# Float32 attention scores in two two-bank PSUM places, the convolution in the recurrent mixer's bank, and one block-diagonal sample operand

## The chip, the cores and the metric

The kernel runs on one core of one Trainium2 chip. The metric is the device time of one execution in microseconds (us); lower is better. The time before is 1830.51 us, the median of three runs.

## What is computed

One layer of a hybrid encoder for 1024 prompt tokens and 64 sample tokens of width 1024. One projection of the normed input (12 groups of 256 columns and 4 more) feeds four mixers of 256 channels each: a gated causal convolution with 31 taps, a "forgetting" softmax attention (fox), a recurrent mixer with a matrix state (HGRN2), and a stick-breaking attention (sb). Then come the output projection, an attention over 256 memory tokens, an MLP with 4096 hidden channels, and a final norm. The two attentions have 4 heads of 64 channels:

```python
def _fox_attend(q, cq, qpos, k, v, ck, kpos):
    s = jnp.einsum('bqhd,bkhd->bhqk', q, k).astype(jnp.float32) * (HEAD_DIM ** -0.5)
    s = s + jnp.swapaxes(cq, 1, 2)[..., :, None] - jnp.swapaxes(ck, 1, 2)[..., None, :]
    s = jnp.where(kpos[None, :] <= qpos[:, None], s, NEG_BIG)
    p = jax.nn.softmax(s, axis=-1)
    return jnp.einsum('bhqk,bkhd->bqhd', p.astype(v.dtype), v)
```

The stick-breaking attention replaces the softmax by a running sum of log-sigmoids from the last key backwards. Prompt queries see the prompt's keys up to their own; the 64 sample queries see 512 cached keys and their own 64.

## The kernel before, in words

**Stages.** The input is transposed to channels first and normed (lines 222 to 278). Then the mixers run (lines 280 to 966). Then come the output projection, the memory attention and the MLP (lines 982 on). All dense products split both operands into two float32r parts, so that one product is three matmuls (`mm3`, L185).

**Lanes.** In the mixer stage four Python generators, the lanes, write the program side by side: `lane_projections` (L641), `lane_attention` (L675), `lane_conv` (L709) and `lane_hgrn` (L789). A step names a nominal cost, and the lane that is furthest behind goes on (L949). This sets the order of the program and the scheduling priorities: the projections' weights and results first, then attention, the recurrent mixer, the convolution, and last the projections' products ("fillers", `products`, L307). A scheduler at build time then fixes the order on each engine by priority among what it holds ready. Each engine executes its own list in order, so an instruction that waits holds up what is behind it on its engine. Tiles of one tag share that tag's places; a new tile waits until an old one's last reader is done. The weights of the next dense products and the stores are issued on SP's queue in the same way.

**Attention** (`attend`, L512). For each pair of heads there are eight blocks of 128 queries; block i has n = 128(i+1) keys. A head's scores are a float32 product of 64 rows (its channels) by up to 512 keys, so n over 512 takes two. Head 0 lies on partitions 0 to 63, head 1 on 64 to 127. Fox adds bfloat16 products for the forget sums (`neg1`, `ckx`), and both add a mask by one more product. The chains `sb_chain` (L467) and `fox_chain` (L480) read the scores from PSUM; `key_T` (L489) transposes the result, and the product with the values follows. Scores lie in one place of one bank (tag "zs") and one of two banks (tag "zl"):

```python
def score_tile(n, h2):
    if n > 512 or h2:
        return ps_zl.tile([P, 1024], F32, name="z", tag="zl")
    return ps_zs.tile([P, 512], F32, name="z", tag="zs")
```

For n up to 512 both heads' products stand next to each other in the program. For n over 512 (blocks 4 to 7) both heads use "zl" in turn: head 1's products follow head 0's chain. The 64 sample queries (L551 to L571) take 512 cached and 64 own keys; each head has its own products, with 64 columns of weights, into its half of the partitions.

**PSUM.** Its eight banks in this stage: two for projections (`ps_mm`), two for "zl", one each for "zs", transposes and value products (`ps_tr`), the recurrent mixer (`ps_hg`) and the convolution with some small transposes (`ps_cv`).

**Convolution** (`lane_conv`). Three chunks of up to 352 prompt tokens and one of 64 sample tokens. In each, two channel tiles are gated and run through 31 taps on DVE (L733, L736). The last chunk of a group transposes its last 30 inputs into `pco` (L743), which is copied out at L747. Then `pme` (L749) sums both channel tiles over the partitions, one matmul for each tile, and `pva` (L757) does the same with the squares.

**Recurrent mixer** (`lane_hgrn`). Six blocks, three for each pair of heads. In each, seven levels (`level`, L827) make decayed keys and queries by way of the tiles `hd` and `hx` (two places each), and the tiles `phhvn`, `pz`, `pd`, `phhkn`, `po`, `pst` and `phm` follow one another in the bank of `ps_hg`.

**After the mixers.** `split_mix` (L968) loads the mixers' outputs from DRAM (`mix_d`) and splits them; the first 512 tokens are loaded early, the others at L1133. `dense_add` (L1026) multiplies them by the output weights into `pa`, the first 512 tokens first.

Of the kernel before, what the change touches and what calls it, by code (L numbers as in the profile page):

```python
# [8 lines left out]
F32 = mybir.dt.float32  # L9
F32R = mybir.dt.float32r  # L10
BF16 = mybir.dt.bfloat16
U8 = mybir.dt.uint8
AF = mybir.ActivationFunctionType
# [4 lines left out]
P = 128  # L18
# [3 lines left out]
SS = 64  # L22
# [9 lines left out]
NEG = -2.0 ** 100       # in bfloat16 too  # L32
# [8 lines left out]
# scheduling priorities: the weights and results of the projections first, their products last, as fillers  # L41
# [3 lines left out]
class Need:  # L45
    """a step of a lane that waits until a projection has been issued"""
# [6 lines left out]
def kernel(ctx: ExitStack, tc: tile.TileContext, *args):  # L53
# [25 lines left out]
    # ---------------------------------------------------------------- constants  # L79
# [27 lines left out]
    # lvl[m][s, blk] = 1 where s lies in the first half of block blk of 2m tokens  # L107
# [31 lines left out]
    # ---------------------------------------------------------------- helpers  # L139
    def rstd_chain(pool, n, mean_sq, tag, scale=1.0, parts=P, out=None):  # L140
        """1/sqrt(mean_sq*scale + eps): exp(-ln/2) and one Newton step."""
# [12 lines left out]
    def softplus_tail(out, z):  # L154
        """out = ln(1 + exp(-|z|))"""
        act(out, z, AF.Abs)
        act(out, out, AF.Exp, scale=-1.0)
        act(out, out, AF.Ln, bias=1.0)

    def sigmoid(out, z):  # L160
        """out = exp(min(z, 0) - ln(1 + exp(-|z|)))"""
        softplus_tail(out, z)
        V.scalar_tensor_tensor(out=out, in0=z, scalar=0.0, in1=out, op0=ALU.min, op1=ALU.subtract)
        act(out, out, AF.Exp)
# [20 lines left out]
    def mm3(ps, w, a, kt=KD, group=0):  # L185
        """ps = W^T a with W and a as pairs of exact float32r parts; a(k) gives the moving pair. With group set, the
        products of that many k stay together once the first is scheduled."""
# [13 lines left out]
    pj_d = dram.tile([12, P, T], F32, name="pj_d")      # cv_a, cv_g, hq, hf, hi, hgate: two tiles each  # L201
# [20 lines left out]
    # ---------------------------------------------------------------- x, channels first. The first norm's gain goes  # L222
    # into the products' operand, its 1/rms, on all partitions in rb, into their results
# [56 lines left out]
    # ---------------------------------------------------------------- projections and mixers  # L280
    ps_zl = mx.enter_context(tc.tile_pool(name="ps_zl", bufs=1, space=PSUM))
    ps_zs = mx.enter_context(tc.tile_pool(name="ps_zs", bufs=1, space=PSUM))
    ps_tr = mx.enter_context(tc.tile_pool(name="ps_tr", bufs=1, space=PSUM))
    ps_hg = mx.enter_context(tc.tile_pool(name="ps_hg", bufs=1, space=PSUM))
    ps_cv = mx.enter_context(tc.tile_pool(name="ps_cv", bufs=1, space=PSUM))
# [21 lines left out]
    def products(work):  # L307
        """the products of one chunk of a projection, as fillers"""
        ps = ps_mm.tile([P, 512], F32, name="pm", tag="mm")
        prio, tc.cur_priority = tc.cur_priority, PR_MM + pending[1]  # L310
        work(ps)
        pending[1] += 24
        tc.cur_priority = prio
        return ps
# [6 lines left out]
    def together(parts, src=w_in, moving=h_at, chunks=CH):  # L321
        """projections, chunk by chunk"""
# [6 lines left out]
    def project_narrow(c0, cols, sink):  # L329
        """projection to a few channels: the k go in turn to the four column groups of the tensor engine, side by side,  # L330
        so that channel c comes in four parts, on partitions c, 32 + c, 64 + c and 96 + c"""
# [11 lines left out]
    def natural(src, j, out_p, out_s, cs, keep=None):  # L343
        """src [128 channels, n] of chunk j -> rows to DRAM and, if asked, to keep [128, 9, 128]."""
# [13 lines left out]
    def memory_kv():  # L358
        """keys and values of the prompt memory: to the outputs, the keys also with channels first"""
# [50 lines left out]
    def project_qkv(kind, hp, cq, ck, cv, cache_k, cache_v, outs):  # L410
        """projections of one head pair as steps; the tiles land in tiles[kind, hp]"""
# [41 lines left out]
    def caches(hp, cache_k, cache_v):  # L453
        """cached keys of one head pair, channels first, and values"""
# [12 lines left out]
    def sb_chain(z, n):  # L467
        """exp(z - sum of softplus(z) over the keys from its own on). v = that sum - z runs backwards through the keys:
        v[j] = (v[j + 1] + z[j + 1]) - log_sigmoid(z[j]). The last key is masked for all: its v is -NEG, its weight 0."""
# [19 lines left out]
    def key_T(p, n):  # L489
        """p [128, n keys] -> [128 keys, n/128, 128]"""  # L490
# [16 lines left out]
    def score_tile(n, h2):  # L507
        if n > 512 or h2:
            return ps_zl.tile([P, 1024], F32, name="z", tag="zl")
        return ps_zs.tile([P, 512], F32, name="z", tag="zs")  # L510

    def attend(hp, kind, mask, chain, cache_k, cache_v, mix_slot):  # L512
# [3 lines left out]
        for i in range(8):  # L516
            n = P * (i + 1)
            # the two heads lie on different rows of the tensor engine: their products go side by side
            zs, aTs = [None, None], []

            def scores(heads):
                for h2 in heads:
                    zs[h2] = score_tile(n, h2)
                for c in range(0, n, 512):
                    for h2 in heads:
                        w = min(512, n - c)
                        mm(zs[h2][:, c:c + w], qT[hd[h2], i * P:(i + 1) * P], kT[hd[h2], c:c + w], True,
                           c + w < n and not fox)
                for h2 in heads:
                    if fox:  # L530
                        for c in range(0, n, 512):
                            w = min(512, n - c)
                            mm(zs[h2][:, c:c + w], neg1[:, 2 * hp + h2], ckx[:, c:c + w], False, c + w < n)
                    mm(zs[h2][:, n - P:n], ident_bf, mask[0], False, True)

            if n <= 512:
                scores((0, 1))
            for h2 in range(2):
                if n > 512:
                    scores((h2,))  # L540
# [12 lines left out]
        z = score_tile(n, 0)  # L553
        for h2 in range(2):
            mm(z[hd[h2], 0:PAST], qT[hd[h2], SP:T], kcT[hd[h2]], True, not fox)
            mm(z[hd[h2], PAST:n], qT[hd[h2], SP:T], kT[hd[h2], SP:T], True, False)
            if fox:
                mm(z[hd[h2], 0:PAST], neg1[:, 2 * hp + h2, 0:SS], ckx[:, SP:SP + PAST], False, True)
                mm(z[hd[h2], PAST:n], neg1[:, 2 * hp + h2, 0:SS], ckx[:, SP + PAST:], False, False)
            mm(z[hd[h2], PAST:n], ident_bf[:, hd[h2]], mask[1], False, True)  # L560
# [12 lines left out]
    # ---- log forget sums, kept as three exact bfloat16 parts so that the score products can take them in  # L573
# [5 lines left out]
    Q.memset(ckx, 0.0)  # L579
    for h in range(4):  # L580
        Q.memset(neg1[32 * h:32 * h + 3, h], -1.0)

# [17 lines left out]
    def ck_cache():  # L600
# [3 lines left out]
        ps = ps_cv.tile([P, 4, P], F32, name="plc", tag="cv")  # L604
# [6 lines left out]
    def sink_f(ps, j):  # L611
# [11 lines left out]
        def later():  # L623
            pl = ps_cv.tile([P, 4, 4], F32, name="plf", tag="cv")
# [15 lines left out]
    # ---- the projections, in the order in which the mixers ask for them  # L640
# [32 lines left out]
    # ---- the two attentions. The query's own log forget sum is the same for every key of a row: the row maximum  # L673
    # takes it out again, so that s + cq - ck - max(s + cq - ck) = (s - ck) - max(s - ck).
# [14 lines left out]
    # ---- convolution, chunk by chunk, with the last 30 gated inputs carried over  # L689
# [11 lines left out]
    ps = ps_cv.tile([P, 4, 64], F32, name="pcw", tag="cv")  # L701
# [7 lines left out]
    def lane_conv():  # L709
        tails = [None, None]  # L710
        for t0, n in [(t, min(CN, SP - t)) for t in range(0, SP, CN)] + [(SP, SS)]:
# [30 lines left out]
            if last:  # L742
                ps = ps_cv.tile([P, G], F32, name="pco", tag="cv")  # L743
# [5 lines left out]
            pm = ps_cv.tile([P, 512], F32, name="pme", tag="cv")  # L749
# [7 lines left out]
            pv2 = ps_cv.tile([P, 512], F32, name="pva", tag="cv")  # L757
# [13 lines left out]
    # ---- HGRN2: blocks of 128 tokens. With DEPTH = 1 the lower bounds are cumsum(softmax) - softmax[0] = 0 over  # L771
    # an axis of one, so that log f = log_sigmoid(z) and k = sigmoid(-z). Within a block the pairs s < t are cut by
    # halving: both sides of a pair take their decay up to the middle of the smallest block of 2m that holds both.
# [5 lines left out]
    # decayed keys, and decayed queries of each head with zeros for the other head's channels  # L779
# [3 lines left out]
    # scores, s on partitions; every s < t is written for each block, and the rest stays zero. The last place is for  # L783
    # the block of 64 tokens
# [4 lines left out]
    def lane_hgrn():  # L789
        state = {}  # L790
        step = 0
        for hp, (t0, n) in [(hp, c) for hp in range(2) for c in ((0, 384), (384, 384), (768, 320))]:
# [34 lines left out]
            def level(m):  # L827
                """decayed keys and queries of one level"""
                nonlocal step
                nn = nf * P if m == 64 else n  # L830
                dd, ex = ht("hd", bufs=2), ht("hx", bufs=2)
# [3 lines left out]
                bv, dv, xv, qv, kv, ykv, q0, q1 = (bl(a) for a in (b, dd, ex, q, kk, yk, yq[:, 0], yq[:, 1]))  # L835
                V.tensor_tensor(out=dv, in0=bv, in1=bv[:, :, m - 1:m].to_broadcast([P, nn // (2 * m), 2 * m]),
                                op=ALU.subtract)
                act(xv[:, :, m:], dv[:, :, m:], AF.Exp)
                act(xv[:, :, :m], dv[:, :, :m], AF.Exp, scale=-1.0)
# [33 lines left out]
            # s = t  # L873
# [6 lines left out]
            # k decayed to the end of its block (tokens on partitions), q decayed from its start  # L880
            ke = ht("hke", "hd", 2)[:, :n]
# [39 lines left out]
            # per-head norm and gate  # L921
# [354 lines left out]
```

## Time and profile before

| | |
|---|---|
| runs | 1829.59, 1830.51, 1832.58 us; median 1830.51 us |
| span of the profiled execution, first to last instruction | 1828.7 us (its own time is not listed apart; the three runs lie 0.9 to 3.9 us above the span) |
| TensorE (PE) busy | 1778.7 us, 97% |
| weight loads (PEld) busy | 1525.0 us, 83% |
| VectorE (DVE) busy | 1028.4 us, 56% |
| ScalarE (ACT) busy | 784.3 us, 43% |
| GpSimd (POOL) busy | 106.0 us, 6% |

How to read it: busy shares are unions of the instructions' times, and the ends of matmuls are modelled, so successive matmuls overlap in the records; what one costs in a stream is the distance from its start to the next one's. A float32 product shows as two matmul records. A tile's name stands on the left of "<-", what it is made from on the right. A wait is the idle time of an engine ahead of an instruction, put down to what came last.

### The profile page before, as it was taken

To read this page: it belongs to the slowest core of one execution; us is meant where nothing else is said; L and a number is where in the kernel's file an instruction comes from. 1 tells how busy PE (TensorE), PEld (TensorE's weight loads), DVE (VectorE), ACT (ScalarE), POOL (GpSimd) and SP (SyncE) were. 2 spreads that over 40 slices of the span, in tenths; PEclk is the share of its full clock that TensorE was granted. 3 is DMA by queue.
4 is the path that set the end of the run, shared out by engine and by line. 5 is a ranking of instruction groups with operands and counts; after the bars stand their busy time and mean duration, and the time that the engine had idled before them with its cause. 6 is when DMAs were issued, how large, how long until landed. Compare 5 with 4: busy or idle time off the path is not lost. (4 is left out here: it accounts for less than half of the span.)

```text
span 1828.7 us, 28923 instructions
## 1 busy us (share of the span) xinstructions
PE 1778.7 (97%) x11379; PEld 1525.0 (83%) x11379; DVE 1028.4 (56%) x2070; ACT 784.3 (43%) x1618; POOL 106.0 (6%) x193
## 2 busy tenths in 40 slices
PE   7999999999999999999999999999999999999997
PEld 6877757776776787988799999999999999999987
DVE  6455579878788875756867764232323232332335
ACT  6464556355446854445555361413131323232233
POOL 3010202000311300000000000000000000000000
PEclk9999999999999999999999999999999999999999
DMA  8221212222233359322322321111111111111212
GB/s 257 76 65 44 58 48 77 63 64 73 68 102 96 103 161 278 99 87 69 104 76 70 104 75 53 40 53 41 42 46 47 47 35 58 35 52 35 59 41 99
DMA packets 224311, 141.76 MB, mean 78 GB/s; under 512 B 14382, under 2 KB 213743, under 8 KB 224175
## 3 DMA queue, kind: packets, MB, share of 16 engines
q1 hardware_dynamic: 223919, 139.90, 25.8%
q8 instruction: 90, 1.47, 0.4%
q14 instruction: 46, 0.38, 0.1%
q0 software_dynamic: 256, 0.01, 0.0%
HBM read 111.97 MB, written 27.87 MB: 76 GB/s over the span
## 5 line engine op out<-in xcount | busy, mean ns | idle before, releaser
L71 PE MATMUL pu<-ap,wh 128*128 128x512 f32 (+2 forms) x1536 | 363.9, 328 | 0.1
L74 ACT ACTIVATE wh<-wr 128x1024 fp32r<-128x1024 f32 (+1 forms) x196 | 169.8, 866 | 431.4 <-PE pdn L71 286.0
L71 PE MATMUL pm<-ap,wh 128*128 128x256 f32 (+2 forms) x1408 | 340.7, 333 | 0.6 <-DVE vT L430 0.3
L71 PEld LDWEIGHTS pu<-ap,wh 128*128 128x128 f32 x1536 | 261.7, 189 | 20.7 <-DVE ap L168 0.3
L71 PEld LDWEIGHTS pm<-ap,wh 128*128 128x128 f32 x1408 | 234.6, 192 | 24.0 <-issue 3.2
L71 PE MATMUL pu<-ap,wl 128*128 128x320 f32 (+2 forms) x768 | 251.2, 327 | 0.0
L168 DVE TENSOR_TENSOR wl<-wr,wh 128x1024 fp32r<-128x1024 f32 (+1 forms) x196 | 193.2, 986 | 97.2 <-ACT wh L74 90.7
L71 PE MATMUL pm<-ap,wl 128*128 128x256 f32 (+2 forms) x704 | 226.9, 322 | 0.0
L1215 DVE TENSOR_TENSOR xT<-xT,pdn 128x512 f32<-128x512 f32 (+2 forms) x192 | 102.1, 532 | 203.0 <-PE pdn L71 203.0
L71 PE MATMUL pa<-ap,wh 128*128 128x256 f32 (+2 forms) x768 | 186.0, 331 | 1.0 <-ACT wh L74 0.6
L71 PE MATMUL pdn<-aq,wh 128*128 128x256 f32 (+1 forms) x896 | 181.2, 295 | 0.0
L71 PEld LDWEIGHTS pu<-ap,wl 128*128 128x128 f32 x768 | 145.3, 189 | 10.2
L71 PEld LDWEIGHTS pdn<-aq,wh 128*128 128x128 f32 x896 | 148.4, 189 | 4.4
L71 PEld LDWEIGHTS pa<-ap,wh 128*128 128x128 f32 x768 | 131.4, 190 | 12.3 <-ACT wh L74 1.4
L71 PEld LDWEIGHTS pm<-ap,wl 128*128 128x128 f32 x704 | 134.4, 191 | 8.3 <-DVE wl L168 0.2
L71 PE MATMUL pdn<-hid,wh 128*128 128x512 f32 x448 | 139.3, 392 | 0.0
L71 PE MATMUL pdn<-aq,wl 128*128 128x320 f32 x448 | 132.6, 296 | 0.0
L71 PE MATMUL pa<-ap,wl 128*128 128x512 f32 (+2 forms) x384 | 126.4, 330 | 0.0
L736 DVE SCALAR_TENSOR_TENSOR y<-ext,cwT,y 128x352 f32<-128x352 f32 (+2 forms) x240 | 113.7, 501 | 2.2
L74 ACT ACTIVATE rl<-pu 128x320 f32<-128x320 f32 (+2 forms) x96 | 44.8, 467 | 150.7 <-PE pu L71 150.7
L168 DVE TENSOR_TENSOR hid<-rl,hid 128x512 fp32r<-128x512 f32 x32 | 22.1, 692 | 136.8 <-ACT hid L74 136.8
L71 PE MATMUL pq<-ap,wh 128*128 128x512 f32 (+2 forms) x384 | 93.1, 331 | 0.0
(310 smaller groups left out, 2795.7 us busy)
## 6 DMA issues: line engine op xcount, KB each, us to landing
wr<-in_w_up_dram SPq DMA_DIRECT2D x36, 512.0 KB
wr<-in_w_down_dram SPq DMA_DIRECT2D x64, 256.0 KB
wr<-in_w_in_dram SPq DMA_DIRECT2D x24, 512.0 KB
wr<-in_w_out_dram SPq DMA_DIRECT2D x16, 512.0 KB
wr<-in_w_mq_dram SPq DMA_DIRECT2D x16, 512.0 KB
wr<-in_w_mo_dram SPq DMA_DIRECT2D x32, 256.0 KB
xt<-in_x_prompt_dram SPq DMA_DIRECT2D x8, 512.0 KB
wr<-in_w_mk_dram SPq DMA_DIRECT2D x8, 512.0 KB
```

The source lines that it names most:

```text
L71: nc.tensor.matmul(out, lhsT=lhsT, rhs=rhs, start=start, stop=stop, **kw)
L74: nc.scalar.activation(out=out, in_=in_, func=func, **kw)
L168: V.tensor_tensor(out=lo, in0=src, in1=hi.bitcast(F32), op=ALU.subtract)
L736: V.scalar_tensor_tensor(out=y[:, :n], in0=ext[:, j:j + n], scalar=cwT[:, ct, j:j + 1], in1=y[:, :n], op0=ALU.mult, op1=ALU.add)
L1215: V.tensor_tensor(out=xs, in0=xs, in1=ps[:, :cn], op=ALU.add)
```

## The change

Comments and doc strings are also removed; those lines are left out here. What remains:

```diff
-    ps_zl = mx.enter_context(tc.tile_pool(name="ps_zl", bufs=1, space=PSUM))
-    ps_zs = mx.enter_context(tc.tile_pool(name="ps_zs", bufs=1, space=PSUM))
+    ps_z = mx.enter_context(tc.tile_pool(name="ps_z", bufs=2, space=PSUM))
     ps_tr = mx.enter_context(tc.tile_pool(name="ps_tr", bufs=1, space=PSUM))
     ps_hg = mx.enter_context(tc.tile_pool(name="ps_hg", bufs=1, space=PSUM))
-    ps_cv = mx.enter_context(tc.tile_pool(name="ps_cv", bufs=1, space=PSUM))
...
+    def score_tile():
+        return ps_z.tile([P, 1024], F32, name="z", tag="z")
...
+            zs, aTs = [score_tile() for _ in range(2)], []
+            for c in range(0, n, 512):
+                for h2 in range(2):
+                    w = min(512, n - c)
+                    mm(zs[h2][:, c:c + w], qT[hd[h2], i * P:(i + 1) * P], kT[hd[h2], c:c + w], True,
+                       c + w < n and not fox)
+            for h2 in range(2):
+                if fox:
+                    for c in range(0, n, 512):
                         w = min(512, n - c)
...
+                        mm(zs[h2][:, c:c + w], neg1[:, 2 * hp + h2], ckx[:, c:c + w], False, c + w < n)
+                mm(zs[h2][:, n - P:n], ident_bf, mask[0], False, True)
             for h2 in range(2):
-                if n > 512:
-                    scores((h2,))
                 p = chain(zs[h2][:, :n], n)
...
+        for sl in hd:
+            act(qbd[sl, sl], qT[sl, SP:T], AF.Copy)
+        z = score_tile()
+        mm(z[:, 0:PAST], qbd, kcT, True, not fox)
+        mm(z[:, PAST:n], qbd, kT[:, SP:T], True, False)
+        if fox:
+            mm(z[:, 0:PAST], neg2[:, hp], ckx[:, SP:SP + PAST], False, True)
+            mm(z[:, PAST:n], neg2[:, hp], ckx[:, SP + PAST:], False, False)
+        mm(z[:, PAST:n], ident_bf, mask[1], False, True)
...
+    neg2 = const.tile([P, 2, P], BF16, name="neg2")
+    Q.memset(neg2, 0.0)
     for h in range(4):
         Q.memset(neg1[32 * h:32 * h + 3, h], -1.0)
+        Q.memset(neg2[32 * h:32 * h + 3, h // 2, (h % 2) * 64:(h % 2 + 1) * 64], -1.0)
+    qbd = const.tile([P, P], F32, name="qbd")
+    Q.memset(qbd, 0.0)
...
-            pm = ps_cv.tile([P, 512], F32, name="pme", tag="cv")
+            pm = ps_hg.tile([P, 512], F32, name="pme", tag="hg")
...
-                dd, ex = ht("hd", bufs=2), ht("hx", bufs=2)
+                ex = ht("hx", bufs=2)
...
-                V.tensor_tensor(out=dv, in0=bv, in1=bv[:, :, m - 1:m].to_broadcast([P, nn // (2 * m), 2 * m]),
+                V.tensor_tensor(out=xv, in0=bv, in1=bv[:, :, m - 1:m].to_broadcast([P, nn // (2 * m), 2 * m]),
                                 op=ALU.subtract)
-                act(xv[:, :, m:], dv[:, :, m:], AF.Exp)
-                act(xv[:, :, :m], dv[:, :, :m], AF.Exp, scale=-1.0)
+                act(xv[:, :, m:], xv[:, :, m:], AF.Exp)
+                act(xv[:, :, :m], xv[:, :, :m], AF.Exp, scale=-1.0)
```

All tiles of `ps_cv` (`plc`, `plf`, `pcw`, `pco`, `pme`, `pva`) move to `ps_hg` with tag "hg" in the way shown for `pme`. The tag "hd" of the recurrent mixer (`hke`, `hsq`, a part of the norm) now has one place. No DMA is added or moved.

## Rows read from the trace of the kernel before

**Rows 1.** The page: busy us (share of the span) and instructions of each engine.

```profile
PE 1778.7 (97%) x11379; PEld 1525.0 (83%) x11379; DVE 1028.4 (56%) x2070; ACT 784.3 (43%) x1618; POOL 106.0 (6%) x193
```

**Rows 2.** Windows, mixer stage: length, busy PE, PEld, DVE, ACT, POOL, clock, DMA, GB/s.

```profile
45.00:690.00 645.00, 618.27 (x4315) 469.78 (x4314) 479.82 (x994) 346.04 (x739) 88.86 (x136) 0.99 0.28 79
```

**Rows 3.** Waits of PE, mixer stage: us in total, times, longest.

```profile
PE z L71 <- DVE sba L475: 3.4, 4, 1.5
...
PE pz L71 <- POOL ky L842: 3.1, 3, 1.4
...
PE pz L71 <- DVE hsc L867: 2.2, 3, 1.4
```

**Rows 4.** Timeline of PE, prompt scores: start, us, what, count of records.

```profile
59.62 0.49 PE L71 MATMUL z<-kT,qT 64*128 64x128 f32 x4
...
70.49 0.91 PE L71 MATMUL z<-kT,qT 64*128 64x384 f32 x2
...
71.72 0.91 PE L71 MATMUL z<-kT,qT 64*128 64x384 f32 x2
...
92.45 1.12 PE L71 MATMUL z<-kT,qT 64*128 64x512 f32 x2
...
94.09 0.48 PE L71 MATMUL z<-kT,qT 64*128 64x128 f32 x2
...
555.48 0.70 PE L71 MATMUL z<-kT,qT 64*128 64x256 f32 x4
...
561.26 0.92 PE L71 MATMUL z<-kT,qT 64*128 64x384 f32 x4
```

**Rows 5.** Timeline of PE, sample scores of sb and fox.

```profile
193.84 1.07 PE L71 MATMUL z<-kv,qT 64*64 64x512 f32 x2
...
195.09 1.07 PE L71 MATMUL z<-kv,qT 64*64 64x512 f32 x2
...
481.95 1.07 PE L71 MATMUL z<-kv,qT 64*64 64x512 f32 x2
...
483.46 0.55 PE L818 MATMUL phhvn<-ident,hv 128*128 128x128 f32 x3
```

**Rows 6.** Instructions on z, last readers: ns min/median/max, first and last start.

```profile
L475 DVE TENSOR_TENSOR_SCAN sba<-z,sba x34: 396/1351/2287, 62.2 to 364.2; 128x127 f32<-128x127 f32 x4, 128x255 f32<-128x255 f32 x4, 128x383 f32<-128x383 f32 x4, 128x511 f32<-128x511 f32 x4
...
L74 ACT ACTIVATE fp<-z,fm x34: 343/742/1122, 390.7 to 658.0; 128x128 f32<-128x128 f32 x4, 128x256 f32<-128x256 f32 x4, 128x384 f32<-128x384 f32 x4, 128x512 f32<-128x512 f32 x4
```

**Rows 7.** Instructions on pco, and timeline of PE: convolution's and recurrent mixer's banks.

```profile
L745 PE MATMUL pco<-ident,ext x4: 284/285/287, 516.0 to 657.2; 128*30 128x128 f32 x4
L747 DVE COPY cvo<-pco x2: 403/403/403, 570.3 to 671.4; 30x256 f32<-30x256 f32 x2
...
574.07 0.70 PE L71 MATMUL pme<-y,ones 128*128 128x320 f32 x2
...
607.84 0.76 PE L71 MATMUL pme<-y,ones 128*128 128x320 f32 x2
...
534.14 0.49 PE L818 MATMUL phhvn<-ident,hv 128*128 128x128 f32 x3
```

**Rows 8.** Timelines of SP, DVE and PE where the mixers end.

```profile
682.29 0.61 SPq L934 DMA_DIRECT2D mix_d<-ho  x1
...
696.92 0.32 SPq L768 DMA_DIRECT2D mix_d<-y  x1
...
709.75 1.42 DVE L168 TENSOR_TENSOR ap<-aqw,ap 128x576 fp32r<-128x576 f32 x2
...
734.01 0.45 PE L71 MATMUL pa<-ap,wh 128*128 128x320 f32 x2
```

**Rows 9.** Taps of y (DVE), nearest rows to the new copies (ACT) and memsets (POOL).

```profile
L736 DVE SCALAR_TENSOR_TENSOR y<-ext,cwT,y x240: 266/556/1245, 305.9 to 682.5; 128x352 f32<-128x352 f32 x60, 128x320 f32<-128x320 f32 x30, 128x64 f32<-128x64 f32 x30
...
L74 ACT ACTIVATE os<-pvs x3: 217/224/224, 374.7 to 667.1; 128x64 f32<-128x64 f32 x3
...
L581 POOL MEMSET neg<- 3x128 bf16 x4 | 0.8, 200 | 0.2
```

More of the change, by code (lines that the diff above doesn't have):

```diff
@@ L505, in key_T @@
         return aT
[L507 to L510, printed above, removed]
+    def score_tile():
+        return ps_z.tile([P, 1024], F32, name="z", tag="z")
     def attend(hp, kind, mask, chain, cache_k, cache_v, mix_slot):
@@ L517, in attend @@
             n = P * (i + 1)
[L519 to L525, printed above, removed]
-                        w = min(512, n - c)
[L527 to L537, printed above, removed]
+            zs, aTs = [score_tile() for _ in range(2)], []
[7 more added lines that the diff above has]
+                    for c in range(0, n, 512):
+                        w = min(512, n - c)
+                        mm(zs[h2][:, c:c + w], neg1[:, 2 * hp + h2], ckx[:, c:c + w], False, c + w < n)
+                mm(zs[h2][:, n - P:n], ident_bf, mask[0], False, True)
             for h2 in range(2):
-                if n > 512:
-                    scores((h2,))
                 p = chain(zs[h2][:, :n], n)
@@ L552, in attend @@
         kcT, vc = caches(hp, cache_k, cache_v)
[L553 to L560, printed above, removed]
+        for sl in hd:
[7 more added lines that the diff above has]
+        mm(z[:, PAST:n], ident_bf, mask[1], False, True)
         p = chain(z[:, :n], n)
@@ L603, in ck_cache @@
         nc.sync.dma_start(out=lc, in_=cache_fox_logf[0, 0].rearrange("(i p) h -> p i h", p=P))
-        ps = ps_cv.tile([P, 4, P], F32, name="plc", tag="cv")
+        ps = ps_hg.tile([P, 4, P], F32, name="plc", tag="hg")
         for j in range(4):
@@ L623, in later @@
         def later():
-            pl = ps_cv.tile([P, 4, 4], F32, name="plf", tag="cv")
+            pl = ps_hg.tile([P, 4, 4], F32, name="plf", tag="hg")
             for i in range(0, n, P):
@@ L700 @@
     nc.sync.dma_start(out=hist, in_=cache_conv[0, 0])
-    ps = ps_cv.tile([P, 4, 64], F32, name="pcw", tag="cv")
+    ps = ps_hg.tile([P, 4, 64], F32, name="pcw", tag="hg")
     for ct in range(2):
@@ L742, in lane_conv @@
             if last:
-                ps = ps_cv.tile([P, G], F32, name="pco", tag="cv")
+                ps = ps_hg.tile([P, G], F32, name="pco", tag="hg")
                 for ct in range(2):
@@ L756, in lane_conv @@
                 act(sq[ct], ys[ct], AF.Square)
-            pv2 = ps_cv.tile([P, 512], F32, name="pva", tag="cv")
+            pv2 = ps_hg.tile([P, 512], F32, name="pva", tag="hg")
             for ct in range(2):
@@ L834, in level @@
                 bl = lambda a: a[:, :nn].rearrange("p (c w) -> p c w", w=2 * m)
-                bv, dv, xv, qv, kv, ykv, q0, q1 = (bl(a) for a in (b, dd, ex, q, kk, yk, yq[:, 0], yq[:, 1]))
-                V.tensor_tensor(out=dv, in0=bv, in1=bv[:, :, m - 1:m].to_broadcast([P, nn // (2 * m), 2 * m]),
+                bv, xv, qv, kv, ykv, q0, q1 = (bl(a) for a in (b, ex, q, kk, yk, yq[:, 0], yq[:, 1]))
+                V.tensor_tensor(out=xv, in0=bv, in1=bv[:, :, m - 1:m].to_broadcast([P, nn // (2 * m), 2 * m]),
                                 op=ALU.subtract)
-                act(xv[:, :, m:], dv[:, :, m:], AF.Exp)
-                act(xv[:, :, :m], dv[:, :, :m], AF.Exp, scale=-1.0)
+                act(xv[:, :, m:], xv[:, :, m:], AF.Exp)
+                act(xv[:, :, :m], xv[:, :, :m], AF.Exp, scale=-1.0)
                 V.tensor_tensor(out=q0[0:64, :, m:], in0=xv[0:64, :, m:], in1=qv[0:64, :, m:], op=ALU.mult)
@@ L879, in lane_hgrn @@
             V.tensor_tensor(out=tv, in0=vT, in1=pd[:, :n], op=ALU.mult)
-            ke = ht("hke", "hd", 2)[:, :n]
+            ke = ht("hke", "hd")[:, :n]
             for g0, gn in groups:
@@ L920, in lane_hgrn @@
             yield 3
-            sq = ht("hsq", "hd", 2)[:, :n]
+            sq = ht("hsq", "hd")[:, :n]
             act(sq, o, AF.Square)
@@ L927, in lane_hgrn @@
             nc.sync.dma_start(out=gT, in_=pj_d[10 + hp][:, t0:t0 + n])
-            r = rstd_chain(hc, n, pm[:, :n], (("hd", 2), ("hx", 2), "hz"), scale=1.0 / HD)
+            r = rstd_chain(hc, n, pm[:, :n], ("hd", ("hx", 2), "hz"), scale=1.0 / HD)
             V.tensor_tensor(out=o, in0=o, in1=r, op=ALU.mult)
```

## The prediction

> **What bounds the kernel now.** I read the page first: TensorE is busy for 97% of the span [rows 1], and no other engine comes near. Then the windows, because the change touches the mixer stage alone: from 45 to 690 us PE is busy for 618 of 645 us [rows 2], so its idle time there is only 27 us. The projections' products fill it up to the end of the stage. So the stage costs what PE has to execute, plus the idle time, unless the end of a lane comes too late. Third, the waits of PE: its idle time is spread over many small waits, of which the score products' wait for the stick-breaking scan is 3.4 us in four times and the recurrent mixer's for its operands a few us [rows 3]. A shorter wait of another engine is worth nothing here; fewer or overlapping matmuls are.
>
> Durations below come from the profiled execution, span 1828.7 us. The median of the runs is 1830.5, so 1.8 us lie around the span. I take the sum off the median.
>
> **Sample operand.** Before, each head has its own set of score products, one after the other: head 0 starts at 193.84, head 1 at 195.09, so a set costs 1.25 us in sb; in fox 481.95 to the next product at 483.46 holds head 1's set, 1.51 us [rows 5]. Afterwards one set with all 128 rows and columns does both. A set's records have the same number of moving columns, so I take the same price. Saved: 2 × 1.25 + 2 × 1.51 = 5.5 us of PE. The zeros cost nothing more as long as a product of 128 rows streams like one of 64; the bound from below is therefore 0 if the full operand took twice as long, from above 5.5. I take 5.5, because the columns are what differ between the prompt's records of 0.48, 0.91 and 1.12 us [rows 4].
>
> **Prompt scores, blocks 4 to 7.** Two heads' products that stand next to each other on PE do run side by side: block 0 has both heads' 128 columns, four records, in 0.49 us, and one head alone takes 0.48; four records of 384 columns take 0.92 and one head alone 0.91 [rows 4]. A pair costs what one head costs. One head's products in blocks 4 to 7 are four of 512 columns and one each of 128, 256, 384 and 512: 5 × 1.12 + 0.48 + 0.70 + 0.91 = 7.7 us by the records (0.70 is a pair's, which is one head's). Four attentions: 30.8 us if every block pairs.
>
> But will they pair? The program order is no guarantee, as blocks 1 to 3 show. They already have a place for each head and both heads' products next to each other in the program. Yet 384 columns of head 0 start at 70.49 and those of head 1 at 71.72, with transposes between. Of the twelve blocks 1 to 3 of the four attentions two pair, at 555.48 and 561.26 [rows 4]. The reason is in the chains: head 0's place comes free when its last reader ends, and head 1's only one such reader later, up to 2.29 us for a scan in sb and up to 1.12 us for an exponential in fox [rows 6]. Head 0's products are ready first, rank above the fillers and go alone. Two places change nothing about that for blocks 4 to 7. Bounds: 0 (no product is added, so no loss) and 30.8. I take the share of the nearest rows, 2 of 12: 5.1 us.
>
> The Trainium skill ("TensorE: Matmul & The Clock Gate", Part 3, Packing small matmuls) says that matmuls on different row groups overlap, with starts about 4 ns apart; taken for every block it makes this term 30.8 us, the second rival below; block 0's row agrees, the ten unpaired blocks show what it needs first. The Trainium skill ("TensorEngine Tiling (Array Packing)", Performance Considerations, PSUM Bottleneck) warns that packing speeds up TensorE but not the emptying of PSUM; by it this term would be 0 and the time 1826.3; ten of the twelve blocks agree, two don't.
>
> **Second place.** With one place for blocks 4 to 7, the next head's scores wait for the previous chain, 3.4 us of PE idle time in four waits [rows 3]. With two, the chain is one head further. I take half, 1.7 us; bounds 0 and 3.4. That attention gets ahead faster gains nothing else: the projections that it needs are PE work too, and it will wait for them.
>
> **One bank for convolution and recurrent mixer.** This is the price. The scheduler gives a free place to whoever is ready, and the convolution holds its tiles for long: `pme` takes its first channel tile at 574.07 and its second at 607.84, 34 us later, because 31 taps of the second lie between, each 0.56 us by the median and last in priority on DVE [rows 7, 9]. `pco` is written from 516.0 on and copied at 570.3, 54 us; the second is written by 657.2 and copied at 671.4, 14 us [rows 7]. In a shared bank the recurrent mixer stands still during such a hold, and its next tile after 516 us is needed at 534.14 [rows 7].
>
> Three things bound what that costs. (1) While it stands still, DVE has only taps and evictions to do, so the holds shrink: between 516.0 and 534.14, 18 us, DVE could do 32 of the third chunk's 62 taps if it did nothing else; I estimate 20 beside its other work, so 40 are left, 22 us, and the recurrent mixer's own first steps need no bank. I put the recurrent mixer's delay at 15 us behind the third chunk and 15 behind the fourth, 30 in all (bounds: 0, and the 54 + 34 + 14 = 102 us of the holds). (2) PE does not starve: fillers and the first 512 tokens' output projection lie behind. What must come in time is the second part of the mix: the recurrent mixer stores last at 682.29, the convolution at 696.92, the splits end near 711.2 (two from 709.75, 1.42 us), and the first product on them starts at 734.01 [rows 8]. So the recurrent mixer may be late by 697 − 682 = 15 and the whole by another 23: 38 us. 30 is under that: cost 0. (3) PE runs its list in order, and products of the recurrent mixer that now wait for the convolution's readers hold up fillers. The nearest rows are the 3.1 and 2.2 us that its products wait today [rows 3]; I take 3, bounds 0 and 8.
>
> **Nothing for the rest.** `hd` and `hx` in one tile: the subtraction of a level now waits for POOL's readers of two levels ago, some half us per level of the recurrent mixer; cover is the same 38 us, and 42 levels at 0.5 would use up to 21 of them. The eight copies into `qbd`, some 0.22 us each like `os<-pvs` [rows 9], are 1.8 us on ACT, busy for 346 of 645 us [rows 2], with fillers on PE meanwhile. Six memsets of about 0.2 us [rows 9] join POOL's start; nothing waits for POOL there but work of the mixers after 45 us; uncovered they are 1.2 us. No DMA moves, on SP or POOL.
>
> **Sum.** −5.5 − 5.1 − 1.7 + 3 = −9.3; 1830.5 − 9.3 = 1821.2 us.
>
> **Rivals.**
> 1. *No pair forms and the shared bank eats the rest.* For: the staggered release [rows 6] and 10 of 12 unpaired blocks. −5.5, no gain from the second place, +4 to +8 of waits: 1827 to 1833, say 1829. That is also the case in which the change doesn't do what it says.
> 2. *All long blocks pair.* For: a pair costs one head [rows 4], and a filler group ahead of the scores may last until both places are free. Against: the same twelve blocks. −5.5 − 30.8 − 1.7 + 3 = −35: 1795.5.
> 3. *Slower: the recurrent mixer arrives too late.* One mechanism: the holds of `pco` and `pme` in its bank, from 516 us on. It decides once its delay is over 38 us; each us beyond is paid at 734 us. For: 102 us of holds, levels that are slower by up to 21, and a chain that is short of DVE. Against: the holds shrink as DVE comes free. With half the holds and half the levels' delay, 51 + 10 = 61: 23 − 9 = +14, 1844; with the full sum of 102 it is +64 − 9 = +55, 1886.
>
> **How the numbers follow.** Forecast 45%, rival 1 18%, rival 2 12%, rival 3 25%. A measurement of this kernel can tell about 0.2%, 3.7 us, from no change: under 1826.9 is faster, over 1834.2 slower. Faster: 43 points of the forecast and all of rival 2, 55%. Same: rival 1 and the rest of the forecast, 20%. Slower: 25%. The forecast alone, with the bounds of pairing (0 to 30.8, mostly under 12) and of the waits (0 to 8), lies between 1812 and 1828. The range reaches to most of rival 3's nearer half and part of rival 2: 1802 to 1844.
>
> **What would show it.** Right: one set of `z<-kv` products for each attention's sample, a gap of 1.2 to 1.5 us closed; few four-record groups among the long blocks, with transposes of head 0 between the heads; waits of `z` on L475 below 3.4; `pco` and `pme` in the recurrent mixer's bank with holds, and its store later than 682 but the first 320-column product of `pa` without a wait and about 9 us before 734. Wrong: many pairs of 512 columns (rival 2); idle PE ahead of `pa` on the split of `aqw`, or a last mixer store after 720 us (rival 3); more idle time of PE ahead of `pz`, `po` and `pme` than the gain (rival 1).

## The result, and the profile after

The changed kernel takes 1880.68 us (median of 4 runs, 1878.28 to 1882.76) against 1830.05 us for the kernel before in the same comparison: a ratio of 1.0276, 95% interval [1.0262, 1.0291]. It is **slower by about 50 us**; the forecast was 1821.2 us, the range 1802 to 1844.

The page of the changed kernel (busy us and share, then the granted clock in 40 slices of 47 us each) answers to [rows 1]:

```profile
PE 1784.7 (95%) x11345; PEld 1532.8 (82%) x11355; DVE 1033.4 (55%) x2070; ACT 781.9 (42%) x1626; POOL 97.9 (5%) x199
...
PEclk9999986999999976999999999999999999999999
```

PE is busy 6 us longer in a span of 1876.5 us that is 48 us longer, and the clock has two dips, in slice 7 (281 to 328 us) and in slices 15 and 16 (657 to 751 us). The windows show what PE did there. First the kernel before (its first row is [rows 2]), then the changed one; the columns are length, busy PE, PEld, DVE, ACT, POOL, clock, DMA, GB/s:

```profile
260.00:330.00 70.00, 65.24 (x433) 47.68 (x434) 62.84 (x128) 40.42 (x76) 12.17 (x23) 0.98 0.27 75
690.00:735.00 45.00, 45.00 (x197) 37.27 (x196) 27.33 (x41) 22.48 (x37) 0.00 (x0) 0.97 0.91 279
```

```profile
45.00:690.00 645.00, 597.97 (x4108) 465.45 (x4116) 452.71 (x920) 328.76 (x710) 65.38 (x113) 0.95 0.28 79
260.00:330.00 70.00, 52.37 (x297) 32.75 (x298) 41.85 (x70) 36.30 (x73) 11.04 (x20) 0.67 0.09 27
690.00:735.00 45.00, 23.80 (x126) 13.81 (x127) 22.66 (x50) 12.77 (x34) 11.91 (x19) 0.50 0.09 26
```

Between 260 and 330 us PE executes 297 matmul records instead of 433. Between 690 and 735 us it is busy for 23.8 of 45 us, where before it had no idle time at all. In both stretches VectorE and ScalarE do less as well: none of the three is overloaded, they wait.

**The first stall: 260 to 326 us.** Instructions of the changed kernel on `plf` (transposes of the forget gate) and on `fl`, its input (ns min/median/max, first and last start), then those on `pm`, the projections' products, between 255 and 326 us:

```profile
L621 PE MATMUL plf<-ident,fl x9: 168/242/264, 326.2 to 332.1; 4*128 4x4 f32 x8, 4*64 4x4 f32 x1
...
L615 DVE SCALAR_TENSOR_TENSOR fl<-fz,fl x3: 388/471/680, 241.4 to 330.0; 4x512 f32<-4x512 f32 x1, 4x256 f32<-4x256 f32 x1, 4x320 f32<-4x320 f32 x1
...
L71 PE MATMUL pm<-ap,wh x8: 278/282/384, 255.2 to 256.5; 128*128 128x256 f32 x8
```

The first `fl` is written at 241.4, but its transposes start at 326.2; in the kernel before they started at 254.3. After 256.6 not one product of a projection starts until 328.5. The kernel before has these rows, on `plf` and, for 260 to 326 us, on `pm`:

```profile
L627 PE MATMUL plf<-ident,fl x9: 168/198/221, 254.3 to 265.3; 4*128 4x4 f32 x8, 4*64 4x4 f32 x1
...
L71 PE MATMUL pm<-ap,wh x136: 279/309/631, 261.7 to 323.7; 128*128 128x256 f32 x48, 128*128 128x320 f32 x48, 128*128 128x512 f32 x40
```

The code gives the link: `fl` lies in the two places (tag "st") through which the projections' results also leave. While `plf` waits for the bank, `fl` can't be given up, the results can't leave, the two PSUM places of `pm` stay full, and PE has no filler.

**The second stall: up to 782 us.** The recurrent mixer's first tile of each block is `phhvn`, the convolution's last of each chunk is `pva`. Both on PE, with first and last start: `phhvn` from 440 us on (blocks 4 to 6) in the kernel before, then `phhvn` and `pva` in the changed one:

```profile
L818 PE MATMUL phhvn<-ident,hv x9: 272/273/328, 483.5 to 614.5; 128*128 128x128 f32 x8, 128*64 128x128 f32 x1
```

```profile
L812 PE MATMUL phhvn<-ident,hv x9: 272/273/445, 632.9 to 721.3; 128*128 128x128 f32 x8, 128*64 128x128 f32 x1
...
L71 PE MATMUL pva<-sq,ones x16: 220/459/543, 404.1 to 631.2; 128*128 128x352 f32 x8, 128*128 128x320 f32 x4, 128*128 128x64 f32 x4
```

Blocks 4 to 6 no longer run beside the convolution but behind it: block 4 begins at 632.9, 1.7 us after the start of the last `pva` of the fourth chunk, and 149 us later than before. Its input `hv` had long been sent for, by the instructions on `hv` (SP) between 440 and 650 us:

```profile
L795 SPq DMA_DIRECT2D hv<-pj_d x1: 320/320/320, 490.3 to 490.3; - x1
```

The waits of PE in the whole execution (total, times, longest) show which chain is then alone. In [rows 3] `pz` had 3.1 and 2.2 and `z` 3.4; now there are

```profile
PE pz L71 <- POOL ky L836: 14.8, 4, 8.4
...
PE pz L71 <- DVE hsc L861: 8.5, 4, 3.2
PE z L71 <- DVE sba L473: 5.7, 5, 3.3
PE phhvn L812 <- DVE ho L927: 5.1, 1, 5.1
```

and the end of the mixers, on SP and on PE, answers to [rows 8]:

```profile
765.53 0.32 SPq L928 DMA_DIRECT2D mix_d<-ho  x1
...
782.09 0.45 PE L71 MATMUL pa<-ap,wh 128*128 128x320 f32 x2
```

The recurrent mixer stores last at 765.5 instead of 682.3, and the first 320-column product of `pa` starts at 782.1 instead of 734.0: 48 us, the whole difference of the spans.

**The theories.** Listed in the order in which the program asks for them, the tiles of the shared bank are: blocks 1 to 3 with `plf` and `plc` near the end of block 3, then all four chunks of the convolution, then blocks 4 to 6. Asking means here the first product or transpose that is written into the tile. The changed kernel's trace serves the bank in this order, tile for tile. So the theory is **order**: the scheduler at build time hands out the places of one tag in program order, and a tile that asks later waits even if its operands are ready and the bank is empty. The rival is the prediction's: a free place goes to whoever is ready, and it is the **length of the holds** that costs. Other rivals put the loss on the score places or on the merge of `hd` and `hx`.

### The profile page after: what moved, and what is told of

It is laid out like the page before. It is cut to its first block, busy times and chain, and to the rows that moved or that the text cites. A ratio compares the mean times of both kernels' runs of the same rounds, so it can differ in the third digit from the quotient of the medians.

```text
span 1876.5 us, 28901 instructions
## 1 busy us (share of the span) xinstructions
PE 1784.7 (95%) x11345; PEld 1532.8 (82%) x11355; DVE 1033.4 (55%) x2070; ACT 781.9 (42%) x1626; POOL 97.9 (5%) x199
```

## The experiments

### One part of the change at a time

**Sample operand (`qbd` and `neg2`) and merge alone**, on the kernel before:

```diff
+    act(qbd[sl, sl], qT[sl, SP:T], AF.Copy)
...
-    mm(z[hd[h2], 0:PAST], qT[hd[h2], SP:T], kcT[hd[h2]], True, not fox)
...
+    mm(z[:, 0:PAST], qbd, kcT, True, not fox)
...
-    dd, ex = ht("hd", bufs=2), ht("hx", bufs=2)
+    ex = ht("hx", bufs=2)
```

> The kernel before with two parts of the change alone: the block-diagonal sample operand (one set of score products for both heads) and, because the operand's two constants need the space, the merge of hd and hx. PSUM stays as it was: one two-bank and one one-bank place for scores, a bank of its own for the convolution. Theory (the loss is in the shared bank): the operand gives its 5.5 us and the merge costs nothing, about 1824.5 us against 1830. Rival (the merge makes the recurrent mixer's levels slow enough to be late): 1840 us or more. Rival (a product of 128 rows and columns takes twice as long, no gain from the operand): 1830 us.

Measured: 1822.0 us, ratio 0.9966 [0.9953, 0.9979], so 6.2 us faster (3.8 to 8.6). The operand pays what was forecast, and the merge costs nothing that shows.

**The shared bank alone**, on the kernel before; `pcw`, `plf`, `plc`, `pco` and `pva` are moved like `pme`:

```diff
-    ps_cv = mx.enter_context(tc.tile_pool(name="ps_cv", bufs=1, space=PSUM))
...
-    pm = ps_cv.tile([P, 512], F32, name="pme", tag="cv")
+    pm = ps_hg.tile([P, 512], F32, name="pme", tag="hg")
```

> The kernel before with one part of the change alone: the convolution's and the forget gate's six PSUM tiles in the recurrent mixer's bank (the freed bank stays empty). Theory (the bank's places are handed out in program order, so that blocks 4 to 6 of the recurrent mixer come after all four chunks of the convolution): the whole loss of the change without its gains, 1885 to 1895 us, and the bank served exactly in the order of the program, block 4's first tile after the last chunk's second moment. Rival (the second place of the scores, their pairing or the merge of hd and hx causes the loss): 1830 to 1838 us.

Measured: 1897.87 us, ratio 1.0378 [1.0364, 1.0392]. This one part costs 69 us, more than the whole change and 3 us more than the theory's upper end. Its `phhvn` from 440 us on and its `pva`:

```profile
L817 PE MATMUL phhvn<-ident,hv x9: 273/273/446, 649.1 to 741.8; 128*128 128x128 f32 x8, 128*64 128x128 f32 x1
...
L71 PE MATMUL pva<-sq,ones x16: 222/458/488, 422.1 to 647.1; 128*128 128x352 f32 x8, 128*128 128x320 f32 x4, 128*128 128x64 f32 x4
```

Again block 4 begins right after the last `pva`. The score places and the merge aren't the cause; the rest of the change gives 17 us back (1897.9 to 1880.7).

### Order or length of the holds

**The forget gate's tiles (`plf`, and `plc` in the same way) elsewhere**, on the changed kernel:

```diff
-    pl = ps_hg.tile([P, 4, 4], F32, name="plf", tag="hg")
+    pl = ps_mm.tile([P, 4, 4], F32, name="plf", tag="mm")
```

> The changed kernel with the forget gate's two PSUM tiles (plf, plc) moved to the two places of the projections' products; the convolution's pcw, pco, pme and pva stay in the recurrent mixer's bank. Theory (program order): plf no longer waits behind block 3 of the recurrent mixer, the products of the projections run on from 260 to 326 us where they stood still, and some 25 us come back: about 1856 us; blocks 4 to 6 still come after the last chunk. Rival (what counts is only how long the convolution holds the bank): plf and plc are short tiles, so no change, 1876 to 1885 us.

Measured: 1850.42 us, ratio 1.0118 [1.0104, 1.0133]: 30 us of the 50 are back, 6 more than expected. The window 260 to 330 us is as it was in the kernel before, clock included:

```profile
260.00:330.00 70.00, 64.78 (x475) 50.30 (x473) 65.63 (x126) 41.47 (x78) 10.50 (x21) 1.00 0.26 73
```

In the changed kernel `plf`, the tile that caused this stall, is held for less than 1 us each time, from its first write to its last reader. It was where it stood, not how long it stayed. Blocks 4 to 6 still come behind the last chunk: block 4 begins at 603.4, after a last `pva` from 599.4 to 602.9.

**The convolution later in the program**, on the changed kernel:

```diff
-             Lane(lane_conv(), 1.0, PR_CONV), Lane(lane_hgrn(), 1.0, PR_HGRN)]
+             Lane(lane_conv(), 4.0, PR_CONV), Lane(lane_hgrn(), 1.0, PR_HGRN)]
```

> The changed kernel with one number changed: the convolution's lane counts its steps four times, so that in the program its chunks 2 to 4 stand behind the recurrent mixer's blocks 4 to 6. Priorities, tiles and the length of each hold are the same. Theory (program order decides): blocks 4 to 6 start near 490 us instead of 633, the last mixer results come 20 to 40 us earlier, 1840 to 1860 us; plf still waits behind block 3, so that the stall between 260 and 326 us stays. Rival (the bank goes to whoever is ready first, and the holds cost the time): the same order of service as in the changed kernel, 1876 to 1885 us.

Measured: 1896.86 us, ratio 1.0377 [1.0363, 1.0392]. The time is a miss, 37 us over the theory's upper end, but the order of service turned round as the theory says: block 4 begins at 501.9, and the last chunk's `pva` comes at 786.3.

```profile
L812 PE MATMUL phhvn<-ident,hv x9: 272/273/273, 501.9 to 638.3; 128*128 128x128 f32 x8, 128*64 128x128 f32 x1
...
L71 PE MATMUL pva<-sq,ones x16: 218/459/486, 410.1 to 786.3; 128*128 128x352 f32 x8, 128*128 128x320 f32 x4, 128*128 128x64 f32 x4
```

Now the convolution is what arrives too late, by the timeline of SP: its last stores start at 792, not at 697.

```profile
792.22 2.00 SPq L762 DMA_DIRECT2D mix_d<-y  x2
```

The expectation had left out what it costs that chunks 2 to 4 then stand behind block 6, one after the other.

**Short holds at the old places**, on the changed kernel; `pco` is asked for and copied for each channel tile, ahead of its taps:

```diff
+    ps = ps_hg.tile([P, P], F32, name="pco", tag="hg")
...
-    for ct in range(2):
-        mm(pm[:, :n], ones, ys[ct], ct == 0, ct == 1)
+    for ct in (1, 0):
+        mm(pm[:, :n], ones, ys[ct], ct == 1, ct == 0)
```

> The changed kernel with short holds and the same places in the program's order: the convolution's means begin with the second channel tile (ready last), and pco becomes one small tile for each channel tile, copied before the taps begin. Each hold of 10 to 36 us of pme and 8 to 30 us of pco becomes one of a few us. Theory (program order decides; the previous run with the convolution's chunks behind block 6 moved block 4 from 633 to 502 us): block 4 still starts only after the fourth chunk's second moment, near 630 us, 1870 to 1883 us. Rival (the length of the holds decides): the recurrent mixer uses the bank between them, block 4 starts before 520 us, 1815 to 1835 us.

Measured: 1880.01 us, ratio 1.0295 [1.0276, 1.0314]: no change. The holds of `pme` are gone: in the changed kernel the second chunk's records lie 17 us apart, here all four stand together, timeline of PE:

```profile
470.72 0.76 PE L71 MATMUL pme<-y,ones 128*128 128x352 f32 x2
487.71 0.92 PE L71 MATMUL pme<-y,ones 128*128 128x352 f32 x2 [0.89 <-DVE y L730]
```

```profile
494.10 1.45 PE L71 MATMUL pme<-y,ones 128*128 128x352 f32 x4 [0.50 <-DVE y L736]
```

And its instructions on `phhvn` from 440 us on and on `pva`:

```profile
L810 PE MATMUL phhvn<-ident,hv x9: 272/273/445, 636.5 to 724.2; 128*128 128x128 f32 x8, 128*64 128x128 f32 x1
...
L71 PE MATMUL pva<-sq,ones x16: 275/457/563, 409.7 to 634.9; 128*128 128x352 f32 x8, 128*128 128x320 f32 x4, 128*128 128x64 f32 x4
```

From 500 to 636 us the holds, each from the first write to the last reader, sum to 23 us, 12 of them one `pva`; the bank is empty for the rest, and still block 4 begins at 636.5, behind the last `pva`. This rules the length of the holds out as what keeps block 4 back.

### The order put right

**Convolution's lane counted twice**, with the forget gate's tiles in `ps_mm`: chunk 3 falls within block 5 and chunk 4 within block 6.

```diff
-             Lane(lane_conv(), 1.0, PR_CONV), Lane(lane_hgrn(), 1.0, PR_HGRN)]
+             Lane(lane_conv(), 2.0, PR_CONV), Lane(lane_hgrn(), 1.0, PR_HGRN)]
```

> The kernel with the forget gate's tiles in the projections' places (1850.4 us), and with the convolution's lane counting its steps twice, so that in the program block 4 stands before the third chunk, the third chunk's tiles within block 5 and the fourth's within block 6, much as the kernel before served its two banks in time. Holds and priorities are the same. Theory (program order): block 4 near 490 us, block 6 done before 700 us, both lanes end within 30 us of each other, 1818 to 1832 us. Rival (any sharing of the bank with holds of 10 to 36 us costs the time whatever the order): 1845 to 1860 us.

Measured: 1825.79 us, ratio 0.9979 [0.9965, 0.9993]. Against 1850.4 the order alone gives 25 us, and the sharing now costs less than the rest of the change gains. The 45 us that were half idle are filled again, and block 4 begins at 472.3, by the window and by the instructions on `phhvn` from 440 us on:

```profile
690.00:735.00 45.00, 44.00 (x217) 36.63 (x217) 32.38 (x50) 24.05 (x41) 0.00 (x0) 1.00 0.76 234
```

```profile
L812 PE MATMUL phhvn<-ident,hv x9: 272/273/301, 472.3 to 626.5; 128*128 128x128 f32 x8, 128*64 128x128 f32 x1
```

**The same with short holds** (the two edits together):

> The run with the forget gate's tiles in the projections' places and the convolution's lane counted twice (1825.8 us), now with the short holds as well. Theory (order first, and once the order is right the remaining holds of 10 to 25 us and what waits behind them cost what is left to the run without any common bank, 16 us): 1812 to 1820 us, better than both kernels. Rival (with the right order the holds lie beside the convolution's own taps and cost nothing; the rest is the order itself, which still ties block 5 to the third chunk): 1822 to 1828 us.

Measured: 1834.87 us, ratio 1.0031 [1.0015, 1.0046], outside both expectations and 9 us slower than with long holds. The edit had also moved requests: the third chunk's first `pco` now stands ahead of block 4 in the program, its second within it. Block 4 waits for it, as its `phhvn` shows:

```profile
L810 PE MATMUL phhvn<-ident,hv x9: 270/273/279, 491.3 to 650.9; 128*128 128x128 f32 x8, 128*64 128x128 f32 x1
```

491.3 instead of 472.3, and the last block's start is 24 us later too (650.9, not 626.5). A shorter hold at an earlier place in the order is a loss, as the theory has it.

**Counted 2.25 times**, on the two kernels just shown, with short and with long holds:

```diff
-             Lane(lane_conv(), 2.0, PR_CONV), Lane(lane_hgrn(), 1.0, PR_HGRN)]
+             Lane(lane_conv(), 2.25, PR_CONV), Lane(lane_hgrn(), 1.0, PR_HGRN)]
```

> The same with the convolution's lane counted 2.25 times: the third chunk's tiles come behind block 6's last scores in the program and the fourth chunk's behind block 6. Theory (program order): block 6 is done about 20 us earlier, the convolution's last store some 15 to 25 us later than with 2.0; 1810 to 1825 us, depending on which lane ends last, with the convolution the last. Rival (order has no more influence): the same as with 2.0 to 2 us, with the same order of service.

> The changed kernel with the forget gate's tiles in the projections' places and the convolution's lane counted 2.25 times, and with its tiles as the change has them (long pme and pco, not shortened). In the program the third chunk's pco and pme come within block 6 and the fourth's behind it; when their turn comes their operands are there, and the holds are short by themselves. Theory (only the order has to fit): 1815 to 1823 us, as with the shortened holds (1820.0), block 4 to 6 without a gap on the bank, better than the kernel before by 5 to 13 us. Rival (the shortened holds were what made 1820): 1826 us or more, like the run with 2.0 and long holds.

Measured: 1819.98 us, ratio 0.9961 [0.9945, 0.9976], with short holds, and 1824.83 us, ratio 0.9968 [0.9958, 0.9979], with long ones, each against its own runs of the kernel before (1828.45 and 1830.02). The second lies between its two expectations, 2 us over the theory's. By the ratios the two are alike. Both are faster than the kernel before by 0.2 to 0.55%, as the sample operand alone is; which of the three is best can't be told apart.

The nine kernels with the shared bank (the changed one and eight of these runs) bear the theory out together: each takes its 95 to 101 tiles in exactly the order of their first products or transposes in the program. One check is missing. The convolution's lane was never counted twice in the kernel before, where nothing is shared, so what the count is worth by itself isn't known.

### What the rest of the change is worth

With the forget gate's tiles in `ps_mm` and without the convolution's other tiles in PSUM nothing shares the bank. The kernel before and the changed one were run in that way, and the changed one also with the products of blocks 4 to 7 written head by head (the last line). `pva`, `pco` and what reads the three are gone like `pme`, so these kernels leave out the convolution's normalization:

```diff
-    pm = ps_hg.tile([P, 512], F32, name="pme", tag="hg")
+    nc.sync.dma_start(out=(conv_s if t0 == SP else conv_p)[0, 0], in_=cache_conv[0, 0])
...
+    for heads in ((0, 1),) if n <= 512 else ((0,), (1,)):
```

> The kernel before with the convolution's PSUM tiles left out: no mean, no second moment and no normalization in its layer norm, and its two state outputs copied from the cache instead of pco; plf and plc in the projections' places. A base for the next run, without any use of a common bank. It saves TensorE 12 small products and 16 products of up to 352 columns: 1815 to 1828 us.

> The changed kernel with the same parts of the convolution left out, so that the recurrent mixer has its bank alone: what is left of the change is the sample operand, the merge of hd and hx, the two two-bank score places and the pairs. Theory (the shared bank is the whole loss, and the scores' second place and the seven 512-column pairs give some 5 to 11 us beside the operand's 6): 10 to 17 us under the run without the change. Rival (pairs and second place give nothing where the stage has no other stall): 6 us under it. Rival (they cost time, by their own waits): level with it or above.

> The changed kernel without the convolution's PSUM tiles and its layer norm's moments (1809.8 us, 17 under the same of the kernel before), with the two heads' products of blocks 4 to 7 written one head after the other, as in the kernel before; both two-bank places stay. Theory (the pairs of blocks 4 to 7 are worth 6 us of TensorE, by the start-to-next times of their records): 1814 to 1817 us. Rival (the second place alone brings the rest, pairs or not): 1808 to 1811 us.

Measured: 1826.83 us without the change, ratio 0.9994 [0.9982, 1.0006]; 1809.78 us with it, 0.9895 [0.9868, 0.9923]; 1808.01 us head by head, 0.9893 [0.9872, 0.9913]. So the rest of the change is worth 17 us, as the bank-only kernel said. But the heads side by side are not what brings it: I counted the records of `z<-kT,qT` that start within a quarter of their predecessor's duration, 34 side by side and 17 head by head (12 in the kernel before), and the sums of all these products' start-to-next times are 71.4 and 76.3 us. These 4.9 us of PE don't show in the time, where the intervals overlap.

Against 1809.8 us the kernels with the order put right (1820.0 to 1825.8) still lie 10 to 16 us higher. What takes these wasn't tried; they also do more work for the convolution.

## Why the prediction was wrong

- **Sample operand:** forecast −5.5 us. The eight records of `z<-kv` that are left (16 before) and the run with that part alone, −6.2 us, agree. Right.
- **Pairs in blocks 4 to 7:** forecast −5.1 us. More pairs formed than 2 in 12, and they save 4.9 us of PE's work; the term's size is right on PE, but no run shows it in the time. The Trainium skill ("TensorE: Matmul & The Clock Gate", Part 3, Packing small matmuls) lets matmuls on different row groups overlap; the 34 records agree, and the time of the run head by head shows that this was not what counted.
- **Second place:** forecast −1.7 us, half of the 3.4 in [rows 3]. Head by head, without the pairs of blocks 4 to 7 and without a shared bank, the change is worth 1826.8 − 1808.0 = 18.8 us; less the 6.2 of the operand, about 12 are left for the second two-bank place, by subtraction and uncertain by some 5. The step failed in size: it priced only the wait of `z` itself and put attention's getting ahead at nothing. The last stick-breaking scan starts at 330.0 there and at 368.0 without the change, so attention is 38 us ahead. How that becomes 12 us wasn't tried.
- **Shared bank:** forecast +3 us, measured +69. The step that failed is the sentence "The scheduler gives a free place to whoever is ready, and the convolution holds its tiles for long". The three points that followed bound what holds cost. With the holds of `pco` and `pme` cut to a few us nothing changed (1880.0); with the long holds, the forget gate's tiles elsewhere and another order the loss went away (1880.7 to 1850.4 to 1825.8). What decides is who asked first in the program. There the lanes' nominal costs place all four chunks ahead of block 4, while the convolution's taps are last in priority on DVE: the recurrent mixer queued behind the work that is done last.
- **A row misread on the way:** the step took 534.14 for the recurrent mixer's next use of its bank after 516 us and so had 18 us in which a hold could shrink at no cost. In the timeline of PE of the kernel before, block 4 still takes tiles in between:

```profile
518.12 0.34 PE L71 MATMUL pst<-hvn,hkn 128*64 128x64 f32 x4
...
525.79 0.81 PE L71 MATMUL phm<-hsq,ones_b 128*128 128x384 f32 x2
```

- **Cover:** the step put the recurrent mixer's delay at 30 us under a slack of 38. The slack was about right, the delay 83 us (682.3 to 765.5), which leaves 45 us by that count; the product at 734.0 came 48 us later. The run with the forget gate's tiles elsewhere agrees: its last store, at 736.0, is 54 us late, 16 over the slack, and the product, at 752.6, is 19 us late.
- **Waits of PE:** fillers held up by products that wait were priced at 3 us. The worse case was not seen: `plf`, a tile held for under 1 us, stopped the fillers themselves through `fl`. That was 30 us, by the run that moved it.
- **Rival 3** had the place of the loss, its threshold and, with the full sum of 102 us of holds, 1886 us. Its mechanism was not the right one: that sum lies near the result by chance, since the delay doesn't come from the holds.
- **Merge, copies, memsets:** forecast 0; the run with operand and merge alone shows no cost.

With the measured terms, 69 for the bank alone and 17 for the rest by the two runs in which nothing is shared, the sum is 69 − 17 = +52 us, against the 50.6 us measured.

## What to carry to other kernels

When two chains that run side by side are put on one buffer, ask in which order the program requests it, not only how long each holds it: here the places of a tag were served in program order, and a chain of high priority queued behind one of the lowest. Write out the two request lists and compare them with the times at which the old trace used the two buffers; where they differ, the difference is the delay. Move the requests, by the order in which the program is generated, before shortening holds, and look for what else a waiting small tile keeps occupied.

## What the runs showed that was not expected

The stalls cost clock as well as idle time. Between 690 and 735 us the granted clock is 0.50, the 1.2 GHz level. It was 1.00 until 677 us and 0.50 from 680 on; PE had no product from 674.6 to 683.0, and then until 728 only the recurrent mixer's, in pieces of 0.5 to 2.6 us between waits. The first of them in the timeline of PE, with the wait before it:

```profile
682.99 1.54 PE L71 MATMUL pz<-qz,ky 128*64 128x128 f32 x6 [8.36 <-POOL ky L836]
```

The same product `pd` of 384 columns took 524 ns by the median in the kernel before and 914 ns here:

```profile
L71 PE MATMUL pd<-hdq,ones_b x4: 486/524/590, 503.4 to 565.8; 128*128 128x384 f32 x4
```

```profile
L71 PE MATMUL pd<-hdq,ones_b x2: 847/914/980, 698.8 to 699.5; 128*128 128x384 f32 x2
```

So here the chain that was left alone ran slower just where everything waited for it. The Trainium skill ("TensorE: Matmul & The Clock Gate", Part 1) says that the throttled clock is the default state and that activity releases it; the trace agrees, with 0.50 here and 0.97 in the same window of the kernel before.
